# Strided attention on one core: loading keys and values from the GpSimd queue instead of the SP queue

## The chip, the cores and the metric

One core of a Trainium2 chip. The metric is device time in microseconds (us), the median over runs of one kernel; single executions are listed where their spread matters. A profiled execution has a span, which is about 1.8 us shorter than its time. A run is called slow where it lies more than 1.5% above the fastest of the same kernel.

## The reference

Every query attends to the 16 positions 0, 64, 128, ... of its head. There are 8 x 12 = 96 heads, 1024 queries each, dimension 64, float32.

```python
attend_positions = np.arange(0, seq, stride)            # 16 of 1024
scores  = einsum('bhqd,bhkd->bhqk', q, k[attend]) / sqrt(dim)
weights = exp(scores - max); weights /= sum(weights) + 1e-10
result[:, :, i, :] = einsum('bhqk,bhkd->bhqd', weights, v[attend])
```

Q and the result are 25.2 MB each, all of which must move. Of K and V only every 64th row is read: 1536 rows of 256 bytes each, 0.39 MB from each tensor.

## The kernel before

The heads are worked on in 24 groups of four. A group's Q is one load of 1 MB and its output one store of 1 MB. Per group, GpSimd casts Q to bf16, VectorE (DVE) transposes it, TensorE (PE) makes scores, ScalarE (ACT) takes the exponential, TensorE makes sums and outputs, and VectorE divides. All transfers are issued by SP in program order on one queue:

```python
kv_src = [[stride * D, P], [2 * HG * SD, NC], [1, D]]    # 128 x 12 pieces of 256 bytes

def load(g):
    qn[g] = qn_pool.tile([P, 32 * D], FP32, name="qn", tag="qn")
    n = P if g < 2 else 32                               # rows that the 1 MB is cut into
    _copy(nc, qn[g], _ap_with(Q, [[HG * SD // n, n], [1, HG * SD // n]], g * HG * SD))

nc.sync.dma_start(k_raw, _ap_with(K, kv_src))
load(0)
nc.sync.dma_start(v_raw, _ap_with(V, kv_src))
for g in range(1, QBUFS):                                # QBUFS = 10
    load(g)
# ... GpSimd: identity, iotas, perm_k, perm_v, then
nc.gpsimd.memset(k_t[:, 8:NG], 0.0)
# ...
keys(0)          # DVE: k_m <- k_raw; PE; ACT: k_t
cast(0)          # GpSimd
transpose(0)     # DVE
scores(0)        # PE, ACT
value_rows()     # DVE: v_bf <- v_raw; PE; DVE: v_rep
values(0)        # GpSimd: vb <- v_rep
# ... then for each group: sums, outputs, store(g), load(g + QBUFS)
```

`n` sets how a Q load is cut: blocks 0 and 1 into 128 rows of 8 KB, later ones into 32 rows of 32 KB. And the first store comes only after keys, values and Q block 0 have all passed through the chain above.

The softmax here doesn't subtract the row's maximum and nothing guards it: scores larger than these inputs give would overflow.

Of the kernel before, what the change touches and what calls it, by code (L numbers as in the profile page):

```python
# [19 lines left out]
def _ap_with(ap: bass.AP, new_ap, extra_offset: int = 0) -> bass.AP:  # L20
    return dataclasses.replace(
        ap, ap=[list(p) for p in new_ap], offset=ap.offset + extra_offset
    )


def _copy(nc, out: bass.AP, in_: bass.AP):

    sides = [
        mybir.BassSymbolicTensorAccessPattern(
            ap=side.ap, dtype=side.dtype, bass_ap=side,  # L30
            is_dma=True, for_custom_bir_dma=True,
        )
        for side in (in_, out)
    ]
    return nc.sync.add_instruction(
        mybir.InstDMACopy(
            name=nc.get_next_instruction_name(), engine=mybir.EngineType.SP,
            ins=sides[:1], outs=sides[1:], queue="qSPDynamicHW",
            mode="Copy",
        )  # L40
    )
# [8 lines left out]
def kernel(  # L50
# [8 lines left out]
    nc = tc.nc  # L59
# [12 lines left out]
    QBUFS = 10  # L72
# [16 lines left out]
    k_raw = const.tile([P, NC, D], FP32, name="k_raw")  # L89
    v_raw = const.tile([P, NC, D], FP32, name="v_raw")  # L90
    kv_src = [[stride * D, P], [2 * HG * SD, NC], [1, D]]
    qn = {}

    def load(g):
        qn[g] = qn_pool.tile([P, 32 * D], FP32, name="qn", tag="qn")
        n = P if g < 2 else 32
        _copy(nc, qn[g], _ap_with(Q, [[HG * SD // n, n], [1, HG * SD // n]], g * HG * SD))

    nc.sync.dma_start(k_raw, _ap_with(K, kv_src))
    load(0)  # L100
    nc.sync.dma_start(v_raw, _ap_with(V, kv_src))
    for g in range(1, QBUFS):
        load(g)


# [227 lines left out]
```

## Time and profile before

| | before |
|---|---|
| time, us | 129.65 (129.57 to 130.0) |
| span of the profile, us | 127.7 |
| DMA queue, share of 16 engines | 96.8% |
| keys landed at, us | 4.9 |
| values landed at, us | 9.2 |
| VectorE's first k_m (needs keys) and v_bf (needs values) start at, us | 7.48 and 11.33 |
| first reciprocal (start of VectorE's steady work), us | 20.65 |
| VectorE's last instruction over at, us | 119.97 |

The engine rows of the page give busy shares; the rows that carry the argument are quoted in the prediction.

Read the table as two chains that run side by side: the transfers, full from 3 to 124 us, and VectorE, which is nearly as full and has to be early enough to keep the stores coming.

### The profile page before, as it was taken

To read this page: it belongs to the slowest core of one execution; us is meant where nothing else is said; L and a number is where in the kernel's file an instruction comes from. 1 tells how busy PE (TensorE), PEld (TensorE's weight loads), DVE (VectorE), ACT (ScalarE), POOL (GpSimd) and SP (SyncE) were. 2 spreads that over 40 slices of the span, in tenths; PEclk is the share of its full clock that TensorE was granted. 3 is DMA by queue.
4 is the path that set the end of the run, shared out by engine and by line. 5 is a ranking of instruction groups with operands and counts; after the bars stand their busy time and mean duration, and the time that the engine had idled before them with its cause. 6 is when DMAs were issued, how large, how long until landed. Compare 5 with 4: busy or idle time off the path is not lost. (4 is left out here: it accounts for less than half of the span.)

```text
span 127.7 us, 1518 instructions
## 1 busy us (share of the span) xinstructions
PE 73.3 (57%) x508; PEld 38.6 (30%) x508; DVE 109.2 (85%) x170; ACT 39.6 (31%) x55; POOL 66.7 (52%) x69
## 2 busy tenths in 40 slices
PE   0006767974476097866675579755567776674000
PEld 0003233441433063333342234432234323342000
DVE  6997468999979987899999999999999999999500
ACT  3003404224244134344424440444431344323000
POOL 8980499675217605387767635787555727000000
PEclk9999999999779855599999965799998559999555
DMA  2999989898998998989989999999999999999981
GB/s 70 380 322 459 482 339 482 349 482 359 462 472 336 503 400 377 505 346 431 493 344 439 454 385 436 441 408 452 426 398 464 385 421 431 426 416 428 421 372 46
DMA packets 7913, 51.23 MB, mean 401 GB/s; under 512 B 3872, under 2 KB 3872, under 8 KB 3872
## 3 DMA queue, kind: packets, MB, share of 16 engines
q1 hardware_dynamic: 7904, 51.12, 96.8%
q8 instruction: 4, 0.07, 0.2%
q14 instruction: 5, 0.04, 0.1%
HBM read 25.95 MB, written 25.17 MB: 400 GB/s over the span
## 5 line engine op out<-in xcount | busy, mean ns | idle before, releaser
L254 DVE TENSOR_TENSOR out_sb<-o_ps,rec 128x512 f32<-128x512 f32 x96 | 59.9, 685 | 4.8 <-PE o_ps L249 2.6
L229 ACT ACTIVATE w<-sc 64x512 bf16<-64x512 f32 x48 | 35.1, 732 | 60.0 <-PE sc L218 56.7
L207 POOL CAST qb<-qn 128x2048 bf16<-128x2048 f32 x24 | 45.5, 1898 | 0.4 <-DMA qn<-in_Q_dram 0.4
L249 PE MATMUL o_ps<-vb,w 128*128 128x256 bf16 x192 | 38.0, 321 | 2.4 <-DVE out_sb L254 1.4
L199 POOL TENSOR_TENSOR vb<-mask,v_rep 128x256 bf16<-128x256 bf16 x24 | 16.1, 670 | 40.3 <-PE o_ps L249 35.4
L218 PE MATMUL sc<-qt,k_t 128*128 128x512 bf16 x96 | 32.7, 472 | 1.5 <-DVE qt L211 1.2
L211 DVE STREAM_TRANSPOSE qt<-qb 128x1024 int32<-128x1024 int32 x24 | 29.7, 1237 | 1.6 <-POOL qb L207 1.6
L249 PEld LDWEIGHTS <-w 128*128 128x128 bf16 x192 | 19.3, 110 | 16.2 <-issue 8.6
L238 PE MATMUL sm<-s_sel,w 128*128 128x4 bf16 x192 | 8.7, 167 | 22.1 <-ACT w L229 22.1
L238 PEld LDWEIGHTS <-w 128*128 128x128 bf16 x192 | 6.9, 100 | 30.1 <-ACT w L229 29.6
L218 PEld LDWEIGHTS <-k_t 128*128 128x128 bf16 x96 | 10.8, 114 | 12.0 <-issue 6.5
L169 PE MATMUL kp<-perm_k,k_m 128*128 128x128 bf16 x24 | 3.1, 311 | 17.5 <-DVE k_m L161 17.5
L242 DVE RECIPROCAL rec<-sm 128x32 f32<-128x32 f32 x24 | 7.8, 326 | 0.3 <-PE sm L238 0.3
L169 PEld LDWEIGHTS <-k_m 128*128 128x128 bf16 x24 | 2.3, 141 | 18.2 <-DVE k_m L161 18.2
L177 ACT CAST k_t<-kp 128x512 bf16<-128x512 f32 x6 | 3.2, 590 | 14.1 <-PE kp L169 14.1
L161 DVE TENSOR_SCALAR k_m<-k_raw,slot_m 128x256 bf16<-128x256 f32 x12 | 6.8, 626 | 0.0
L192 DVE CAST v_rep<-vp 128x384 bf16<-128x384 f32 x4 | 2.2, 558 | 2.6 <-PE vp L188 2.6
L135 POOL MEMSET k_t<- 128x4608 bf16 x1 | 3.9, 3938 | 0.0
L145 DVE TENSOR_SCALAR s_sel<-col,slot_f 128x4 bf16<-128x4 int16 x1 | 3.2, 3155 | 0.1
L188 PE MATMUL vp<-v_bf,perm_v 128*128 128x384 bf16 x4 | 2.0, 489 | 0.8 <-DVE v_rep L192 0.6
L177 ACT ACT_TABLE_LOAD x1 | 1.3, 1283 | 2.1 <-DVE k_t L129 2.1
L129 DVE MEMSET k_t<- 128x1152 uint32 x1 | 1.0, 1018 | 1.0 <-PEq L314 1.0
(17 smaller groups left out, 6.3 us busy)
## 6 DMA issues: line engine op xcount, KB each, us to landing
qn<-in_Q_dram SPq DMA_DIRECT2D x24, 1024.0 KB, 13.9
out_dram<-out_sb SPq DMA_DIRECT2D x24, 1024.0 KB, 12.0
k_raw<-in_K_dram SPq DMA_DIRECT2D x1, 384.0 KB, 4.1
v_raw<-in_V_dram SPq DMA_DIRECT2D x1, 384.0 KB, 7.2
```

Source lines behind the costliest of these rows:

```text
L161: nc.vector.tensor_scalar(out=k_m[:, 4 * m : 4 * m + 4, :, h], in0=kr, scalar1=slot_m[:, h : h + 1], scalar2=None, op0=ALU.mult,)
L169: nc.tensor.matmul(kp[:, i, :, f], lhsT=k_m[:, 4 * m + 2 * u + i, f].rearrange("p h q -> p (h q)"), rhs=perm_k.rearrange("p c a b k -> p c ...
L177: nc.scalar.copy(_ap_with(dst, [dst.ap[0], [KW, 8], [32, 4], [1, NK]], extra_offset=NK), kp.rearrange("p i c f (s k) -> p (i c f) s k", s=4),)
L199: nc.gpsimd.tensor_tensor(out=vb[g], in0=mask, in1=v_rep[:, g // 2, g % 2].unsqueeze(1).to_broadcast([P, 4, D]), op=ALU.mult,)
L207: nc.gpsimd.tensor_copy(out=qb[g], in_=qn[g])
L211: nc.vector.transpose(qt[g].bitcast(I32), qb[g].bitcast(I32))
L218: nc.tensor.matmul(sc, lhsT=k_t[:, g, f, NK * (1 - e) : NK * (1 - e) + P], rhs=_ap_with(q, [q.ap[0], [2 * D, 8], [16 * D, 2], [2, 32]], ex ...
L229: nc.scalar.activation(out=_ap_with(wa, [wa.ap[0], [P, 8], [1, 2], [2, 32]], extra_offset=64 * a), in_=sc[64 * a : 64 * a + 64].rearrange( ...
L238: nc.tensor.matmul(sm[:, :, i], lhsT=wt[g][:, i], rhs=s_sel, start=True, stop=True)
L242: nc.vector.reciprocal(rec[g], sm.rearrange("p b i e -> p b (i e)"))
L249: nc.tensor.matmul(ps[:, :, i], lhsT=wt[g][:, 2 * c + i], rhs=vb[g].rearrange("p s d -> p (s d)"), start=True, stop=True,)
L254: nc.vector.tensor_tensor(out=out_sb[g][:, :, 4 * c : 4 * c + 4], in0=ps.rearrange("p b i (e d) -> p b (i e) d", e=2), in1=rec[g][:, :, 4 ...
```

## The change

The intent: keys and values no longer stand in SP's queue around the first Q block; a second queue, GpSimd's, loads them at the same time.

```diff
-    nc.sync.dma_start(k_raw, _ap_with(K, kv_src))
-    load(0)
-    nc.sync.dma_start(v_raw, _ap_with(V, kv_src))
-    for g in range(1, QBUFS):
+    nc.gpsimd.dma_start(k_raw, _ap_with(K, kv_src))
+    nc.gpsimd.dma_start(v_raw, _ap_with(V, kv_src))
+    for g in range(QBUFS):
         load(g)
```

## The prediction

> **What bounds the kernel now.** I read the page first, then the windows by stage, then the waits of the DMA queue, then the first 12 us of the timeline. The page's slices of the span show the DMA engines full from the second slice to the last but one, with VectorE (DVE) close behind:
>
> ```profile
> DVE  6997468999979987899999999999999999999500
> POOL 8980499675217605387767635787555727000000
> DMA  2999989898998998989989999999999999999981
> ...
> q1 hardware_dynamic: 7904, 51.12, 96.8%
> ```
>
> The row to look at is DMA: one digit 2, then nines and eights, then 8 and 1. All 51.12 MB go through one queue, whose packets cover 96.8% of the 16 engines' time. The windows give the rate by stage (columns: busy time and count of PE, PEld, DVE, ACT, POOL, then PE clock, DMA share, GB/s):
>
> ```profile
> 0.00:2.00 2.00, 0.00 (x0) 0.00 (x0) 0.95 (x1) 0.00 (x0) 1.40 (x12) 1.00 0.03 8
> 2.00:3.00 1.00, 0.00 (x0) 0.00 (x0) 0.89 (x3) 0.85 (x1) 1.00 (x8) 1.00 0.66 155
> ...
> 40.00:120.00 80.00, 52.16 (x391) 28.06 (x389) 76.16 (x121) 28.89 (x40) 40.98 (x34) 0.84 1.01 423
> ...
> 123.00:124.00 1.00, 0.00 (x0) 0.00 (x0) 0.00 (x0) 0.00 (x0) 0.00 (x0) 0.50 0.86 360
> 124.00:125.00 1.00, 0.00 (x0) 0.00 (x0) 0.00 (x0) 0.00 (x0) 0.00 (x0) 0.50 0.45 188
> 125.00:126.00 1.00, 0.00 (x0) 0.00 (x0) 0.00 (x0) 0.00 (x0) 0.00 (x0) 0.50 0.18 74
> ```
>
> From 40 to 120 us the engines move 423 GB/s at a share of 1.01: full. The check is a sum: 48 blocks of Q and output, 1.049 MB each, 50.33 MB in all, at 423 GB/s are 119.0 us; the keys and values (0.79 MB at the 301 GB/s of the stage in which they move) are 2.6 us; the start is about 2 us, the landing of the last store about 2 us: 125.6 of the 127.7 us. So the transfers set the time, from the first packet to the last. The chain of waits does not say so, as it follows instructions and ends with DVE's last multiplication; the queue's own waits say it: the program's end waited 6.1 us for the last store.
>
> VectorE is the second bound, and it is close: 76.16 of these 80 us. Its last instruction is over at 119.97 us and the last store is issued then. That store lands 6.7 us later, the shortest of all 24 (median 12.0). With the queue empty I estimate 4.0 to 5.3 us for such a store: 2.5 us for 1.049 MB at 423 GB/s, plus 1.5 us (some 1.1 us from the first issue at 0.74 us to data in the row 2 to 3 us, 0.4 us to land), or plus 2.8 us, which is what the keys' load has over its transfer (4.1 us to landing, less 384 KB at 301 GB/s). So VectorE has **1.4 to 2.7 us of slack** before it, and not the queue, sets the end; I take 2.2, because shares of 0.45 and 0.18 after 124 us show that a few late engines set the end, and those have the most work queued.
>
> The start is where the change acts:
>
> ```profile
> 0.73 0.20 POOL masks.py:197 MEMSET identity<- 128x128 bf16 x1 [0.29 <-POOLq L314]
> ...
> 3.21 3.94 POOL L135 MEMSET k_t<- 128x4608 bf16 x1
> 7.54 2.04 POOL L207 CAST qb<-qn 128x2048 bf16<-128x2048 f32 x1 [0.39 <-DMA qn<-in_Q_dram]
> ...
> 4.01 3.15 DVE L145 TENSOR_SCALAR s_sel<-col,slot_f 128x4 bf16<-128x4 int16 x1
> ...
> 7.48 2.77 DVE L161 TENSOR_SCALAR k_m<-k_raw,slot_m 128x256 bf16<-128x256 f32 x4
> 10.17 1.23 DVE L211 STREAM_TRANSPOSE qt<-qb 128x1024 int32<-128x1024 int32 x1
> ```
>
> GpSimd (POOL) works without a gap from 0.73 to 7.15 us, waits 0.39 us for Q block 0, and casts it. VectorE's tiny s_sel (512 elements) takes 3.15 us and ends just when GpSimd's fill of k_t ends, and the four k_m take 2.77 us, where later ones take 0.34 each: VectorE waits for GpSimd there. So **GpSimd's work before its first cast is the head of VectorE's chain**, and the keys, landed by about 4.9 us, are not.
>
> **What the Trainium skill says.** "DMA: Bandwidth & Descriptors", section "Issuing engines are not separate DMA queues": transfers from any queue run on the same 16 engines and interleave, and a second issuer saves only issue time. The trace of before has one data queue and fills the engines, so it agrees as far as it goes. The same page, "Latency and other measured facts", gives about 1 us to the first byte for a DMA from GpSimd and 600 ns from SP; the trace has about 1.1 us for SP, so the measurement decides. The same page, "Anatomy of one DMA", calls descriptor generation "small, variable" and says many can be emitted before it shows; no run here shows it yet. "SBUF — State Buffer", "Who interferes with whom": VectorE and GpSimd share a pair of SBUF ports under an exclusive lock, and the loser blocks. The s_sel of 3.15 us agrees.
>
> **The change part by part.**
>
> 1. Removed from SP: two issues, 0.43 and 0.59 us. Q block 0 is now first, at 0.74 instead of 1.23 us. SP issues its first ten loads far ahead of the transfers, so this is worth at most the slow rise of the keys' small pieces at the head of the stream: the row 2 to 3 us is full to 0.66, and a Q block at the head might save 0.3 us of it.
>
> 2. Moved, not removed: 0.79 MB in 3072 pieces of 256 bytes. They take the same time on the same engines, now interleaved with Q. DMA total: 0.
>
> 3. Added to GpSimd, ahead of everything it does: two DMA issues whose descriptors it makes in software, 1536 pieces each. The order of its instructions confirms that they stand before the identity and all constants, with nothing taken out. No row of this profile has a duration for it. The lower end is about 1 us each (the skill's first-byte figure, as an estimate); the upper end I put at 4 ns a piece, 6 us each. I choose 2.5 us each, five times the 0.5 us that SP's issue of the same pieces takes in the timeline; this factor is a judgment. **5 us on GpSimd.**
>
> 4. Given back: Q block 0 no longer lands behind the keys, so the 0.39 us wait goes. With GpSimd late, s_sel can slip between its small copies instead of standing behind the k_t fill; if so, the k_m may be done before the first cast ends and the first transpose starts about 1 us sooner after the cast. I count 0.5 of that. Delay of VectorE's chain: 5.0 - 0.4 - 0.5 = 4.1 us.
>
> 5. The load itself: the keys would have descriptors at about 3.3 us, and land by about 8 us behind interleaved Q blocks; the values by about 12. The k_m would want them at about 12, the values at about 15. Neither waits.
>
> 6. VectorE's delay goes through to its end, as it idles for under 5% of the later stages: its last instruction moves from 119.97 to about 124.1 us. Does the queue run dry in between? The first store is issued at 23.6 us, when ten Q blocks (10.5 MB, 25 us at 423 GB/s) are still moving until about 30 us, so a delay of 4 us leaves it full. Later a group takes VectorE 3.98 us (1.24 + 0.32 + 2.48 with overlaps) and the engines 4.95 us for its load and store, so the backlog grows again until the loads end. Only the tail is exposed: 4.1 - 2.2 of slack = 1.9 us.
>
> Sum: 129.64 + 1.9 - 0.3 = 131.2 us; I say **131.2**.
>
> **The rivals.**
>
> A. It is hidden: descriptor generation costs about 1 us a DMA. Then the delay is 2 - 0.9 = about 1 us, below the slack, and the time is 129.3 to 129.8. For it: the full DMA row, and the skill's wording. Against it: 1536 pieces are far more than an ordinary block's 128.
>
> B. GpSimd becomes the bound of the start: 4 ns or more a piece, 12 us in all. Then VectorE is late by some 11 us, the queue runs dry before the first store at about 34 us, and the time is 129.64 + 11 - 2.2, about 138. For it: it is a software loop, and the eight constants' copies show that a GpSimd instruction of hardly any data takes some 0.15 us. Against it: the skill's wording.
>
> C. A gain: the 256-byte pieces overlap with 8 KB pieces and the stream gets shorter by up to the head's 1 us. Time 128.7. Against it: every later row is already at 420 GB/s, and no engine is idle to overlap on.
>
> D. The small pieces cost more from descriptors that lie in memory. Twice their present time would add 2.6 us to a full stream: 132. It would show as longer packets on the second queue.
>
> **Range and chances.** The spread is nearly all in step 3. At 2 us on GpSimd the time is 129.5, at 5 it is 131.2, at 7 it is 133.5, at 12 it is 138. The 2% mark is 132.2, reached at about 6 us. I give 0.42 to slower by over 2% (B, D, and the upper part of my own estimate), 0.55 to within 2%, and 0.03 to faster. Range 128.9 to 138.0.
>
> **What would show it right or wrong.** Step 3: the start of the identity's fill on GpSimd, 0.73 us now, about 5.7 predicted. Step 4: the duration of s_sel, under 1 us if it slips in, 3 if not. Step 5: no wait of k_m for k_raw. Step 6: VectorE's last multiplication ending at about 124 us, the first store issued at about 27.7, the last store landing about 4.5 us after its issue instead of 6.7, and DMA shares of 0.9 or more until then. Step 2: small packets that keep their share of time. The prediction is wrong if GpSimd starts its constants before 2.5 us or after 8 us, if the delay of VectorE is made up later, or if the DMA row has a new gap before 100 us.

## More of the kernel before

The start of VectorE's steady work, from the timeline of VectorE (start, duration, instruction, in us):

```profile
11.33 0.51 DVE L184 CAST v_bf<-v_raw 128x768 bf16<-128x768 f32 x1
20.65 0.32 DVE L242 RECIPROCAL rec<-sm 128x32 f32<-128x32 f32 x1
```

## The result, and the profile after

| | before | after |
|---|---|---|
| time with the prediction's runs, us | 129.65 (129.57 to 130.0) | 136.59 (134.41 to 137.31) |
| time in a later batch, us | 129.92 (129.61 to 130.15) | 137.30 (136.65 to 137.49) |
| ratio of fast runs, first batch | 1 | 1.043 (95% interval 1.031 to 1.056) |
| ratio of fast runs, later batch | 1 | 1.056 (1.054 to 1.058) |

A ratio is the mean time of one kernel's fast runs over that of the other's fast runs of the same rounds, so it is not quite the ratio of the medians. In the first batch two of the four runs (136.93 and 137.31) counted as slow, because the fastest (134.41) was so far below; the later batch is the cleaner one. By the medians of all runs the change costs 6.9 and 7.4 us, about 7; by the two fast runs of the first batch alone it costs 5.6.

The page of the changed kernel (second profile, span 135.5 us), to be read against the rows in the prediction:

```profile
DVE  6300602669999689979999999999999999999740
...
DMA  3999998991999899989998998999899899998875
GB/s 68 405 380 440 376 353 377 435 445 48 310 365 467 327 428 445 382 370 314 370 438 356 435 464 375 431 493 428 363 457 455 370 414 426 423 423 353 356 327 232
...
q1 hardware_dynamic: 4800, 50.33, 91.6%
q0 software_dynamic: 224, 0.79, 1.9%
```

VectorE's row has two holes that were not there: slices 3 and 4 (6.8 to 13.6 us) read 0, slices 6 and 7 (16.9 to 23.7 us) read 0 and 2. The DMA row has a 1 in the tenth slice (30.5 to 33.9 us, 48 GB/s), where the kernel before had an 8: the ten Q blocks are in and no store has been issued yet. And q0, the GpSimd queue, has few packets: 224, of which the trace's packet records show 192 of 4096 bytes and 32 of 4 bytes. So 16 pieces of 256 bytes are put into one packet, six packets per DMA engine for the keys and six for the values. In the kernel before each of the 3072 pieces was a packet of its own.

The start, from the timelines of GpSimd and VectorE (start, duration, instruction, and the idle time in front of it with what ended it):

```profile
1.27 1.19 POOL L99 DMA_DIRECT2D k_raw<-in_K_dram  x1 [0.82 <-POOLq L313]
2.46 1.02 POOL L100 DMA_DIRECT2D v_raw<-in_V_dram  x1
3.47 0.22 POOL masks.py:197 MEMSET identity<- 128x128 bf16 x1
...
9.90 1.88 POOL L206 CAST qb<-qn 128x2048 bf16<-128x2048 f32 x1
...
4.66 0.23 DVE L144 TENSOR_SCALAR s_sel<-col,slot_f 128x4 bf16<-128x4 int16 x1
...
14.37 1.14 DVE L160 TENSOR_SCALAR k_m<-k_raw,slot_m 128x256 bf16<-128x256 f32 x4 [8.96 <-DMA k_raw<-in_K_dram]
15.43 1.24 DVE L210 STREAM_TRANSPOSE qt<-qb 128x1024 int32<-128x1024 int32 x1
22.18 0.56 DVE L183 CAST v_bf<-v_raw 128x768 bf16<-128x768 f32 x1 [5.51 <-DMA v_raw<-in_V_dram]
...
30.11 0.32 DVE L241 RECIPROCAL rec<-sm 128x32 f32<-128x32 f32 x1
```

GpSimd is done with both issues at 3.5 us. VectorE has all its constants by 5.4 us and then stands still for 8.96 us until the keys land, at about 14.3 us instead of 4.9, and again for 5.51 us until the values land, at about 22.1 instead of 9.2. The first reciprocal starts at 30.11 us instead of 20.65. These two waits are the loss.

The same stretches in the windows, before and then after (the last three columns are the TensorE clock, the DMA share and GB/s):

```profile
30.00:36.00 6.00, 2.42 (x22) 1.80 (x22) 5.73 (x10) 1.89 (x4) 2.50 (x2) 0.78 0.93 389
36.00:120.00 84.00, 54.96 (x412) 29.58 (x410) 79.38 (x126) 30.35 (x42) 43.23 (x35) 0.85 1.01 425
```

```profile
30.00:36.00 6.00, 4.29 (x35) 1.84 (x34) 5.79 (x11) 2.62 (x4) 5.49 (x5) 0.70 0.51 203
36.00:120.00 84.00, 59.61 (x399) 31.81 (x398) 79.09 (x125) 29.92 (x42) 46.54 (x38) 0.63 0.99 406
```

From 36 to 120 us VectorE is as busy as before (79.09 us against 79.38), only later. The lower TensorE clock in the second of these profiles (0.63 against 0.85) is not the reason: the first profile of the changed kernel has 0.85 in this window too, with 79.35 us of VectorE and 407 GB/s. VectorE's last instruction is over at 130.34 us, and the last store then lands 4.2 us after its issue, the shortest of all stores: the queue in front of it was empty. In the kernel before the shortest was 6.7. So in this profile the end is set by VectorE. The other two profiles of this design are less clear: VectorE ended at 128.98 us (the first profile) and at 128.19 us (the variant with GpSimd's fill moved, below), and the last store landed 5.2 and 5.9 us after its issue. The three spans lie within 0.5 us of each other, so the queue still has a part in the end.

### The profile page after: what moved, and what is told of

Same layout as the page of the kernel before. It is cut to its first block, busy times and chain, and to the rows that moved or that the text cites. A ratio compares the mean times of both kernels' runs of the same rounds, so it can differ in the third digit from the quotient of the medians.

```text
span 135.2 us, 1519 instructions
## 1 busy us (share of the span) xinstructions
PE 71.6 (53%) x508; PEld 38.0 (28%) x508; DVE 104.9 (78%) x170; ACT 39.6 (29%) x55; POOL 68.7 (51%) x71
## 5 line engine op out<-in xcount | busy, mean ns | idle before, releaser
L248 PE MATMUL o_ps<-vb,w 128*128 128x256 bf16 x192 | 36.8, 312 | 3.1 <-DVE out_sb L253 2.2
L217 PE MATMUL sc<-qt,k_t 128*128 128x512 bf16 x96 | 31.7, 460 | 1.4 <-DVE qt L210 1.2
L248 PEld LDWEIGHTS <-w 128*128 128x128 bf16 x192 | 18.8, 108 | 16.6 <-issue 8.5
L237 PEld LDWEIGHTS <-w 128*128 128x128 bf16 x192 | 6.9, 99 | 30.6 <-ACT w L228 29.8
L160 DVE TENSOR_SCALAR k_m<-k_raw,slot_m 128x256 bf16<-128x256 f32 x12 | 4.9, 467 | 8.5 <-DMA k_raw<-in_K_dram 8.5
L183 DVE CAST v_bf<-v_raw 128x768 bf16<-128x768 f32 x1 | 0.6, 561 | 5.5 <-DMA v_raw<-in_V_dram 5.5
L187 PEld LDWEIGHTS <-perm_v 128*128 128x128 bf16 x4 | 0.5, 126 | 6.0 <-issue 4.9
## 6 DMA issues: line engine op xcount, KB each, us to landing
qn<-in_Q_dram SPq DMA_DIRECT2D x24, 1024.0 KB, 13.6
```

Of the source, the lines that this page charges most:

```text
L160: nc.vector.tensor_scalar(out=k_m[:, 4 * m : 4 * m + 4, :, h], in0=kr, scalar1=slot_m[:, h : h + 1], scalar2=None, op0=ALU.mult,)
L217: nc.tensor.matmul(sc, lhsT=k_t[:, g, f, NK * (1 - e) : NK * (1 - e) + P], rhs=_ap_with(q, [q.ap[0], [2 * D, 8], [16 * D, 2], [2, 32]], ex ...
L237: nc.tensor.matmul(sm[:, :, i], lhsT=wt[g][:, i], rhs=s_sel, start=True, stop=True)
L248: nc.tensor.matmul(ps[:, :, i], lhsT=wt[g][:, 2 * c + i], rhs=vb[g].rearrange("p s d -> p (s d)"), start=True, stop=True,)
```

## The experiments

Three theories.

**A, turns.** Each DMA engine serves the two queues in turns, one packet each. The Trainium skill has this rule, and the prediction passed over it: "DMA: Bandwidth & Descriptors", section "Queues, rings and completion order", says that an engine round-robins between the rows it has work for, at packet granularity. A packet of keys then waits for one Q packet, which from block 2 on is 32 KB and takes 1.22 us in the trace. Six turns of 1.22 us plus 0.17 us for the small packet are 8.3 us; the two profiles of the changed kernel show 7.6 and 8.0 us from the first keys' packet (6.2 us) to the keys' landing, and 7.8 and 7.9 more to the values'. The sum is rough, and for the keys it agrees partly by chance. In the packet records of the second profile 73 small packets start before 10 us, and 100 of the 113 Q packets that start from 6 to 10 us are still of 8 KB. From 10 to 20 us 118 small packets start against 99 Q packets, and a Q packet takes 1.3 to 1.45 us there instead of 1.22. And a load has landed when the slowest engine is done: the first of the 16 reported the keys at 10.3 us, the last at 14.3.

**B, GpSimd's time.** The two issues take 2.2 us and push GpSimd's other work back by 2.7 us; this is what the prediction was about.

**C, the path.** The software-generated queue is slow by itself.

All eleven kernels gave correct results. Their times are compared with the kernel before in the same batch: 129.87 us (129.54 to 130.03) for the first eight, 129.92 us for the last three.

### Q cut into 8 KB rows

```diff
-        n = P if g < 2 else 32
+        n = P if g < QBUFS else 32
```

> The changed kernel with the first ten Q loads cut as 128 rows of 8 KB instead of 32 rows of 32 KB. Theory A (the two queues take turns packet by packet on each DMA engine, so each of the six 4 KB packets that an engine holds of the keys waits for one Q packet: 1.22 us at 32 KB, 0.31 us at 8 KB): keys land 6 x 0.48 = about 3 us after their first packet at 6.2 us, so about 9.2 us instead of 13.8; values about 12 us instead of 21.6; VectorE waits less than 1.5 us for either; time 129 to 131. Theory B (GpSimd's 2.7 us of issuing is what delays everything): no change, 134.4 to 137. Theory C (the software-generated queue is slow by itself): keys still land after 13 us, time 134 to 137.

Measured: 130.57 us (130.25 to 131.06), ratio 1.0057 (1.0025 to 1.0089). Nothing about keys, values or GpSimd was touched, and 6 of the 7 us are gone.

```profile
11.68 1.14 DVE L160 TENSOR_SCALAR k_m<-k_raw,slot_m 128x256 bf16<-128x256 f32 x4 [6.27 <-DMA k_raw<-in_K_dram]
15.21 0.56 DVE L183 CAST v_bf<-v_raw 128x768 bf16<-128x768 f32 x1 [1.25 <-DMA v_raw<-in_V_dram]
```

The keys landed at 11.6 us and the values at 15.2: the direction and the time as expected, the landings later than the 9.2 and 12 that I had worked out. The values' six turns took 3.6 us, 0.60 each, against 0.31 + 0.17 = 0.48: while they shared the engines the Q packets took 0.39 to 0.45 us instead of 0.31. On the first turns, for the keys, both kinds of packet took longer than usual, 0.9 us a turn. The expectation that VectorE would wait under 1.5 us for the keys was wrong too: the bracket counts from 5.4 us, when it had nothing else to do.

This B cannot explain, as GpSimd does the same work, nor C. The turns can be counted. Packets that started in each microsecond, from the trace's packet records:

```text
                         8    9   10   11   12   13 us
8 KB variant: keys/values 31   28   22   26   28   28
              Q, 8 KB     27   27   29   28   24   26
```

One for one, summed over the 16 engines, as the records do not name the engine. From 6 to 8 us it was not yet so: 26 small packets against 65 of Q.

### Q cut into 16 KB rows

```diff
-        n = P if g < 2 else 32
+        n = P if g < 2 else 64 if g < QBUFS else 32
```

> The changed kernel with Q loads 2 to 9 cut as 64 rows of 16 KB: the middle dose between 8 KB (values landed at 15.2 us, 130.57 us) and 32 KB (21.6 us, 136.59 us). Turn by turn, a packet of the values waits 0.61 us instead of 0.31 or 1.22: keys land at about 12.3 us, values at about 17.2, time 131.5 to 133.5. If the packet size of Q acted in another way than by turns (a threshold between 8 and 32 KB), it would be like one of the two ends.

Measured: 132.14 us (131.28 to 133.34), ratio 1.0205 (1.0153 to 1.0258); against the 2% mark that is unclear, and the slowest of the four runs (133.34) counts as slow.

```profile
12.20 1.14 DVE L160 TENSOR_SCALAR k_m<-k_raw,slot_m 128x256 bf16<-128x256 f32 x4 [6.79 <-DMA k_raw<-in_K_dram]
17.65 0.56 DVE L183 CAST v_bf<-v_raw 128x768 bf16<-128x768 f32 x1 [3.16 <-DMA v_raw<-in_V_dram]
```

Keys at 12.1, values at 17.6: within half a microsecond of the expectation. From 8 to 16 to 32 KB a turn of the values takes 0.60, 0.92 and 1.30 us, and the kernel 130.57, 132.14 and 136.59 us. Between these three sizes there is no threshold; the size of the other queue's packets is the dose.

### The delay on GpSimd alone

```diff
 (in the kernel before, first on GpSimd)
+    nc.gpsimd.memset(k_t[:, 8:19], 0.0)
     identity = const.tile([P, P], BF16, name="identity")
```

> The kernel before, with a fill of 3168 elements (about 2.7 us) put ahead of everything on GpSimd: the delay of the two issues alone. Theory A: the delay is 2.7 - 0.4 - up to 1 for the small operations that now slip in = 1.3 to 2.3 us, at or under the slack of 2.2 us of VectorE at the end; time 129.5 to 130.3. Theory B: about 136.

Measured: 130.06 us (129.86 to 130.72), ratio 1.0023 (0.9992 to 1.0054).

```profile
4.56 0.23 DVE L146 TENSOR_SCALAR s_sel<-col,slot_f 128x4 bf16<-128x4 int16 x1
...
5.24 1.13 DVE L162 TENSOR_SCALAR k_m<-k_raw,slot_m 128x256 bf16<-128x256 f32 x4
...
22.51 0.32 DVE L243 RECIPROCAL rec<-sm 128x32 f32<-128x32 f32 x1
```

The fill took 2.74 us, as long as the two issues' push. With the keys on time, s_sel slips in between GpSimd's small copies (0.23 us instead of 3.15) and the k_m are done before the k_t fill begins. VectorE's chain is 1.86 us late (22.51 against 20.65), and that is under its slack. B falls.

### Both loads on ScalarE's hardware queue

```diff
-    nc.gpsimd.dma_start(k_raw, _ap_with(K, kv_src))
-    nc.gpsimd.dma_start(v_raw, _ap_with(V, kv_src))
+    nc.scalar.dma_start(k_raw, _ap_with(K, kv_src))
+    nc.scalar.dma_start(v_raw, _ap_with(V, kv_src))
```

> The changed kernel with both loads issued from ScalarE's hardware queue instead of GpSimd's: no software descriptors, nothing on GpSimd. Theory A, with the hardware queue's packets of 256 bytes as in the kernel before (96 an engine for the keys): each takes a turn against a Q packet, the ten Q loads give only 32 packets an engine, so the keys land only when the ten Q loads are through, at about 33 us, and the values at about 35; time about 150 to 158. Theory B and C: nothing is left of the cost, keys land by 7 us, time 129 to 130.

Measured: 139.35 us (138.1 to 139.89), ratio 1.0746 (1.0717 to 1.0776): slower than the changed kernel, although no software makes descriptors and GpSimd starts its constants at 0.73 us again.

```profile
20.88 1.14 DVE L160 TENSOR_SCALAR k_m<-k_raw,slot_m 128x256 bf16<-128x256 f32 x4 [13.33 <-DMA k_raw<-in_K_dram]
23.09 0.52 DVE L183 CAST v_bf<-v_raw 128x768 bf16<-128x768 f32 x1
```

So C falls as the main cause. The size of the effect I had wrong: I expected the keys at 33 us and a time of 150 to 158, and they landed at 20.8. The packet records say why:

```text
                      4    5    6    7    8    9   10  ...  18   19   20   21 us
256-byte pieces      117   48   63   53   51   42   16  ...  15  533  933  230
Q packets             37   48   49   51   50   28   16  ...  15    0    0    0
```

While Q is there, a turn carries one piece of 256 bytes against one Q packet (8 KB up to 9 us, 32 KB after it). At 19 us Q stops, and the rest of the pieces pass in 3 us. Q stopped because SP's seventh Q load reuses the keys' completion semaphore: this trace has eight semaphore numbers for these transfers, taken in turn, of which keys and values hold two and the first six Q loads the rest. SP waited 16.2 us for the keys before it issued the seventh. I had counted on all ten. Turns of about one for one are seen at three sizes of the Q packets and on both kinds of queue.

### Q from block 2 on held back until keys and values have landed

```diff
 (in the changed kernel, shortened)
-    for g in range(QBUFS): load(g)
+    load(0); load(1)
+    nc.scalar.copy(qn[2][:, 0:1], k_raw[:, 0, 0:1])      # load(2) must wait for both
+    nc.scalar.copy(qn[2][:, 1:2], v_raw[:, 0, 0:1])
+    for g in range(2, QBUFS): load(g)
```

> The changed kernel, where Q loads 2 to 9 wait until keys and values have landed (two one-column copies on ScalarE from k_raw and v_raw into the third Q buffer). Only Q blocks 0 and 1 with 8 KB packets compete. Theory A: keys land at about 9 us or earlier, values at about 11, a gap of about 2 us in the stream before Q block 2, time 129.5 to 132. Theory C: keys land as late as before, 13 us or more, and the time is 137 or more because Q waits as well.

Measured: 133.48 us (133.46 to 133.73), ratio 1.0282 (1.0263 to 1.0301), above the expected 129.5 to 132. The values came at 12.0 us as theory A wants (11 expected), the keys only at 10.7. But the stream stopped:

```profile
10.00:11.00 1.00, 0.00 (x0) 0.00 (x0) 0.18 (x1) 0.19 (x1) 1.00 (x2) 1.00 1.08 229
11.00:12.00 1.00, 0.00 (x0) 0.00 (x0) 1.00 (x2) 0.00 (x0) 0.85 (x1) 1.00 0.09 16
12.00:13.00 1.00, 0.15 (x2) 0.16 (x3) 1.00 (x4) 0.19 (x1) 0.00 (x0) 1.00 0.00 0
13.00:14.00 1.00, 0.88 (x8) 0.61 (x6) 1.00 (x2) 0.51 (x2) 0.00 (x0) 1.00 1.00 262
```

Two microseconds at 16 and 0 GB/s, and the rest of the 3.6 us in the slow microseconds around them. VectorE's chain is 2.5 us late, little more than its slack; this time the queue itself lost the time, as it is full from then to the end.

### No Q at all until keys and values have landed

```diff
 (as above, but the two copies write into qn[0], and no Q load precedes them)
```

> The changed kernel, where no Q load at all is issued before keys and values have landed (the two one-column copies now write into Q buffer 0). It separates two reasons for the late first packet of the software queue (6.2 us, although GpSimd is done with the keys' descriptors at 2.45 us). If Q packets already queued on the engines hold it up: first keys' packet at about 3 to 4 us, keys landed by 5.5, values by 6.5, time about 131. If the software path itself takes so long from descriptors to first packet: first packet at about 6 us, keys landed at about 8, values at 9, Q starts at 10 and the time is about 134.

Measured: 133.99 us (two runs, 133.93 and 134.05), ratio 1.0317.

```profile
2.00:3.00 1.00, 0.00 (x0) 0.00 (x0) 0.89 (x3) 0.02 (x1) 1.00 (x2) 1.00 0.00 0
3.00:4.00 1.00, 0.00 (x0) 0.00 (x0) 0.63 (x2) 0.00 (x0) 0.93 (x3) 1.00 0.89 66
4.00:6.00 2.00, 0.00 (x0) 0.00 (x0) 1.04 (x5) 0.00 (x0) 2.00 (x15) 1.00 0.99 260
```

The first keys' packet starts at 3.1 us instead of 6.2, 0.7 us after GpSimd is done with the keys' descriptors. So the late first packet, too, comes from Q, but turns do not explain it: in turns from the start it would wait for one Q packet of about 0.3 us, not 3 us. What holds it back until 6.2 us was not tested. Keys landed at 6.4 and values at 7.9 us, between my two alternatives (5.5 and 6.5, or 8 and 9), so the software path is slower than SP's by itself: 5.2 us from issue to landing, where SP's took 4.1. That is a small part of the changed kernel's 13.0 us: 1.9 us from the issue to the first packet are there without Q as well, 3.1 are its late start beside Q, and 8.0 are the turns. The time matched the other alternative, since Q now starts after 9 us.

### Half of the change: only the values on GpSimd

```diff
     nc.sync.dma_start(k_raw, _ap_with(K, kv_src))
     load(0)
-    nc.sync.dma_start(v_raw, _ap_with(V, kv_src))
+    nc.gpsimd.dma_start(v_raw, _ap_with(V, kv_src))
```

> Half of the change: keys stay first on SP, only the values go to GpSimd. Keys land at 4.9 us as before. Turns: the values' first packet at about 5 to 6 us, six turns partly against 8 KB packets and partly against 32 KB ones, landed at 11 to 14 us; VectorE wants them at about 12, so a wait of 0 to 2 us, and 1.1 us of delay on GpSimd; all of it near the slack: 129.6 to 130.8. If the values' lateness were harmless and the keys' the whole cost, the same; if the values' were the larger part, 133 or more.

Measured: 129.97 us (129.94 to 130.03), ratio 1.0008 (0.9992 to 1.0024): the same. The values are now the first six packets on the second queue, many of whose turns fall against 8 KB packets; they landed at 11.1 us, and v_bf starts at 12.64 without a wait. Here the second queue as such costs nothing. Its cost is the lateness of what the chain is waiting for.

### The same kernel again, and GpSimd's large fill moved

```diff
 (in the changed kernel)
-    nc.gpsimd.memset(k_t[:, 8:NG], 0.0)       # before keys(0)
     cast(0)
+    nc.gpsimd.memset(k_t[:, 8:NG], 0.0)
     transpose(0)
```

> The changed kernel once more, unedited: for more times of it and a second profile, as its four runs lay between 134.41 and 137.31 us. By the turns, keys land at 13 to 14.5 us and values at 20.5 to 22.5 again, and the time lies in the same range; if keys or values land elsewhere by some us, the spread of the times comes from there.

> The changed kernel with GpSimd's 3.94 us fill of the second part of k_t moved behind its first cast: GpSimd reaches the cast about 3.9 us sooner. If GpSimd's work still bounds the start of the changed kernel: 3 us or more faster, 133 or less. If the landing of keys and values bounds it (theory A): the same as the changed kernel, 134.4 to 137.3.

Measured: 137.30 us unedited (its profile is the one shown above) and 136.81 us (135.43 to 137.04), ratio 1.0501 (1.0455 to 1.0547), with the fill moved. GpSimd reached its first cast at 6.19 us instead of 9.90, 3.7 us sooner, and it bought about half a microsecond at most: the keys landed at 14.2 us and VectorE waited 8.88 us for them as before. GpSimd is not on the path that sets the start of the changed kernel. Keys and values landed within 0.5 us of each other in the three profiles, which are all of runs above 136.7 us. Where the 134.41 us run got its 2 us from stays open: no profile caught such a run.

### The same move in the kernel before

> The same move in the kernel before, where GpSimd's work is the head of VectorE's chain: VectorE gets 1 to 3 us ahead. If the transfers set the time, as the prediction has it, that buys nothing: 129.4 to 130.0. If VectorE's chain set it, 127 to 128.5 and a kernel better than both.

Measured: 129.82 us (129.36 to 129.96), ratio 0.9985 (0.9966 to 1.0004): the same. GpSimd's first cast then had to wait 4.4 us for Q block 0 and the first reciprocal came at 21.27 us, no earlier than before. Later VectorE got ahead and ended at 118.43 us, 1.5 us before the kernel before, and the last store landed 8.6 us after its issue at the least, instead of 6.7. VectorE's gain went into a longer queue: the transfers set the end.

### Q block 0 ahead of keys and values, on SP alone

```diff
-    nc.sync.dma_start(k_raw, _ap_with(K, kv_src))
     load(0)
+    nc.sync.dma_start(k_raw, _ap_with(K, kv_src))
     nc.sync.dma_start(v_raw, _ap_with(V, kv_src))
```

> The kernel before with the order on SP changed to Q block 0, keys, values: no second queue, only the head of the stream is a block of 8 KB packets. It tests the gain of 0.3 us that the prediction gave to this part of the change. Keys land at about 7 us, just when VectorE wants them (7.5). Time 129.2 to 129.6, so a ratio of 0.997 to 1.000.

Measured: 130.44 us (130.28 to 130.58), ratio 1.0044 (1.0030 to 1.0059): not a gain of 0.3 but a loss of 0.6 us. VectorE starts its steady work at 20.85 us, as before. The windows of this kernel, and then of the kernel before:

```profile
6.00:8.00 2.00, 0.00 (x0) 0.00 (x0) 2.00 (x1) 0.00 (x0) 2.00 (x2) 1.00 1.33 241
```

```profile
6.00:8.00 2.00, 0.00 (x0) 0.00 (x0) 1.97 (x5) 0.00 (x0) 1.61 (x2) 1.00 1.29 301
```

The two rows are not like for like: by the packet records the first window holds small pieces alone, and the second also holds 27 Q packets of 8 KB. What stands is the sum over the first 10 us, 237 against 262 GB/s; the missing 0.25 MB are 0.6 us at 423 GB/s. A small piece took 18 ns up to 6.5 us in this kernel and about 25 ns from 7 us on; in the kernel before it took 18 ns up to 7 us and 21 to 25 ns after, where fewer were left (959 against 1427). Whether the order of the loads or something else makes the late pieces slower was not tested.

No version beat the kernel before. The stream of transfers is its bound, and none of the variants made that stream shorter.

## Why the prediction was right or wrong

The measured 136.59 us lies inside the stated range, near its upper end. That is luck: the story that led to 131.2 was wrong, and rival B, which gave the upper end, had another cause.

- **The bound, and the slack of VectorE (right).** I took 2.2 us. Several runs now make VectorE late by different amounts; the table sets the delay of its first reciprocal against the extra time in the same batch:

| run | first reciprocal later by, us | time longer by, us | difference |
|---|---|---|---|
| values only | 1.31 | 0.10 | 1.2 |
| delay on GpSimd alone | 1.86 | 0.19 | 1.7 |
| 8 KB rows | 2.56 | 0.70 | 1.9 |
| 16 KB rows | 4.78 | 2.27 | 2.5 |
| the change, first batch | 8.97 | 6.94 | 2.0 |
| the change, later batch | 9.46 | 7.38 | 2.1 |
| ScalarE's queue | 11.76 | 9.48 | 2.3 |

Delays under 2 us are nearly free, and beyond that most of the delay is paid. The delays are of single profiled runs and the times are medians of all runs; with the spans of the profiled runs in place of the medians, the differences are 0.8 to 3.2 us. Two kernels are left out because their stream of transfers was itself stopped: with Q held back from block 2 on, 2.53 us later and 3.61 longer, and with no Q at first, 5.03 later and 4.12 longer.

- **Step 1, a gain of 0.3 us at the head (there, but worth nothing).** Over its first 10 us the changed kernel moved 282 GB/s and the kernel before 262, which is 0.5 us of full transfers; by 30 us this was lost (360 against 376 GB/s). Q block 0 first on SP alone lost 0.6 us, but there the two small-piece loads also followed each other.
- **Step 2, the transfer itself unchanged (right for the bytes; it left out the order).** The pieces were regrouped into packets of 16, whose share of the engines' time is only 1.9%. But the time of all these packets rose, from 96.8% of 127.7 us to 91.6 + 1.9% of 135.5 us, which is 123.6 to 126.7 us: Q packets took longer while they shared the engines.
- **Step 3, 5 us on GpSimd (mis-sized).** The issues took 1.19 and 1.02 us; the identity's fill moved from 0.73 to 3.47 us, so the delay was 2.7 us, not 5. The lower end of my own span, 1 us a DMA, was the truth, and the factor of five that I chose had no ground.
- **Step 4, s_sel slips in (right).** It took 0.23 us. With the keys on time the delay of the chain would be 1.9 us, as the delay on GpSimd alone shows.
- **Step 5, "Neither waits." (the step that failed).** I put the keys at 8 us and the values at 12; they landed at 14.3 and 22.1. I counted bytes, not turns: six packets an engine, each of which takes turns with Q packets of 0.3 us at first and 1.2 to 1.45 us later, after a first packet that started only at 6.2 us. VectorE waited 8.96 and 5.51 us.
- **Step 6 (mechanism right, fed with a wrong number).** VectorE's delay went through to its end (130.34 us), and the last store landed 4.2 us after its issue; 4.5 was predicted. That the queue would not run dry before the first store was wrong at a delay of 9.5 us: the first store was issued at 33.05 us and the stream was down to 203 GB/s from 30 to 36 us.
- **Rival A** had GpSimd's cost right, and nearly the time that this cost alone gives (129.3 to 129.8 forecast, 130.06 measured with the fill). **Rival B** had the time nearly right (138) for the wrong reason; the fill put on GpSimd refutes it. **Rival C** did not come, and **D**, costlier small pieces, is not the cause: by the packet records the small packets took 2.6 us of the 16 engines' time (1.9%), and in the kernel before 3.7. (The prediction's 2.6 us for the kernel before came from a window in which Q packets moved too.)

Worked again with what the runs show: 9.0 to 9.5 us of delay from the two landings, less the 2.2 us of slack that I took, is 6.8 to 7.3 us; the medians gave 6.9 and 7.4, the fast runs of the first batch alone 5.6.

## What to carry to other kernels

Where one queue already fills the engines, as here (96.8%), a second queue changes who goes first. A small load that the whole chain waits for belongs at the head of the one full queue, where its bytes are served in order; on a second queue it got about one packet for every packet of the bulk stream in these runs, so that an estimate of the time from its first packet to its landing is (its packets per engine) times (the duration of one packet of each queue). The wait for the first packet, 3 us here, comes on top. Before moving such a load, count those packets; if it must go on a second queue, cut the competing transfers into small rows while it is under way.

## What the Trainium skill lacked or had wrong

- "DMA: Bandwidth & Descriptors", "Issuing engines are not separate DMA queues" and the row on spreading DMAs over queues in "Rules for kernel authors": they say that a second queue only saves issue time. Here it cost 7 us, as it changed the order: keys landed at 14.3 us instead of 4.9. A warning beside these two passages and the arithmetic of turns (0.60, 0.92 and 1.30 us a turn against Q rows of 8, 16 and 32 KB) are missing.
- The same page, "Queues, rings and completion order": a packet is given as typically about 9 to 17 descriptors. On the GpSimd queue 16 pieces of 256 bytes made a packet, which fits; on the SP and ScalarE queues each piece of 256 bytes was a packet of its own, and took a turn of its own (on ScalarE's queue 48 to 63 pieces a microsecond against 48 to 51 Q packets of 8 KB).
- The same page, "Anatomy of one DMA": no figure for how long GpSimd is held by descriptor generation. Here 1536 pieces held it for 1.19 and 1.02 us.
- The same page, "Latency and other measured facts": about 1 us to the first byte on the GpSimd path. With no other traffic the first packet started 1.9 us after the issue began and the 0.39 MB landed after 5.2 us, against 4.1 us from SP.
- No page says that 256-byte pieces on one queue change their time within a kernel: 18 ns each at first, and about 25 ns after 7 us, in both orders tried on SP. The cause is open.
